# A hybrid short-convolution and SSD trunk: split parts of weight sums kept in DRAM, another order of pairs, two pools exchanged

## The chip, the cores and the metric

The kernel runs on one core of one Trainium2 chip. Time is the device time of an execution in microseconds (us); less is better. Single executions come from the hardware profiler, whose span covers the program from its first to its last instruction.

## The reference

One layer over an input of 2048 positions by 1024 features, float32:

```python
h = rmsnorm(x, norm_mix_w)
proj = einsum("btd,dc->btc", h, w_in)               # 1024 x 5648
u_b, u_c, u_h, z, xbc, dt_raw = split(proj)
y_a = u_b * causal_dwconv(u_c * u_h, short_conv_w)  # 3 taps
xbc = silu(causal_dwconv(xbc, conv_w, conv_b))      # 4 taps
y = ssd_scan(xs, softplus(dt_raw + dt_bias), -exp(a_log), bm, cm) + d_skip * xs
y_b = grouped_rmsnorm(y * silu(z)) * ssd_norm_w
x = x + concat(y_a, y_b) @ w_out                    # 2048 x 1024
h = rmsnorm(x, norm_mlp_w)
x = x + square(relu(h @ w_up)) @ w_down             # 1024 x 4096 x 1024
out = rmsnorm(x, final_norm_w)
```

## The kernel before

**Products.** All large matrix products are made in pairs of output blocks by a scheme with seven products in place of eight (two by two blocks, as Strassen and Winograd have it). `chain` (L272) runs one pair: it goes through the seven products b11, t1, t2, b21, t3, b22, t4, each 4 blocks deep and each block as three matmuls (L297 to L299), because every float32 operand is cut into a high and a low part of type float32r: high times high, high weights times low data, low weights times high data. A product is thus 12 matmuls of 128x512. The results gather in the PSUM tiles px, py and pw and leave through `evict`.

**Weights.** A pair needs four weight operands as (high, low): the block `r0`, the sums `s12` and `s34`, and half of `r1` (`a22`). `combine` (L254) forms the sums on DVE from two loaded blocks (tag `wraw`, 3 buffers) and cuts each with `split_w`: ScalarE (ACT) casts to `whi` (L113), VectorE (DVE) subtracts to `wlo` (L114). `whi` and `wlo` have 4 buffers each, so operand i of the next pair takes the buffer of operand i of this one once PE has done with it. b11 and b21 read operand 0, t1 and t2 operand 1, t3 and b22 operand 2, t4 operand 3. `chain` pulls the next pair's weights from a generator: its loads at t1, two operands after b21, one after b22, one after t4.

**Two halves.** The sequence is worked through as two halves of 1024 positions with the same weights. In the first half (about 75 to 460 us) 20 pairs named in `PAIRS` are projected, and `combine` also stores the two sums (512 KB each) in DRAM, `sums_d`. In the second half (about 460 to 1290 us) come the four output pairs o0 to o3, the 22 pairs of `LATER` (those of `PAIRS`, and z0 and z2), and eight more output pairs. `weights` (L1019) loads r0, s12, s34 and a22 for a pair of `PAIRS`, and cuts all four by `split_w`; z0 and z2 go through `combine`.

**What a pair is followed by.** An x pair has two convolutions of 4 taps (`conv`, three 128x1024 passes on DVE each, and SiLU on ACT), a ch pair a short convolution into a tile `cc`, a b pair a product with two `cc` tiles and sums of its output, a z pair SiLU alone.

**The scan beside it.** `Scan.run` is a generator that yields small steps; `second_half` pulls one to three at each product, so the 32 chunks of the state-space scan run between the products. Its tiles come from the pool `sp1`; `dec` (512 KB, loaded from rd_d at L1613) has one buffer, is changed by ACT (L1673, L127) and DVE (L1679) and read by 16 matmuls into `yd` (L1698). Each change between SiLU and exponent costs ACT a table load.

**Memory and order.** Pools are laid one above the other; a pool that opens where another has closed waits tile by tile for the old tiles' last readers and writers. The first half's pool of temporaries, `pu0`, holds `ea`, `eb` and such (tag `e`) lowest, then other tiles and `cc`, and above it lie the pools of the sums and of raw data. The second half's opens `ut` (4 KB a partition), then `pu1` (tags `cc` and `e`, about 30 KB), then `sp1` (about 27 KB). The first tiles taken from `pu1` are the residual inputs `x` of o0 (L952), to which L985 adds the products. The framework puts the instructions of each engine into an order by its own estimate of when each can run; at run time every engine goes through its list in that order. Nearly all DMAs are issued by SP.

Of the kernel before, what the change touches and what calls it, by code (L numbers as in the profile page):

```python
# [11 lines left out]
F32 = mybir.dt.float32  # L12
# [4 lines left out]
P = 128  # L17
# [6 lines left out]
KD = D // P  # L24
# [15 lines left out]
def trunk(ctx: ExitStack, tc: tile.TileContext, x, x_tok, w_in, w_dt, w_out, w_up, w_down, cvec, hrow, out):  # L40
    nc = tc.nc
# [27 lines left out]
    rd_d = [dram.tile([NC * 16, 2, P], F32, name=f"rd_d{b}") for b in range(NB)]  # L69
    NQ = NF // 2  # L70
    hid_d = [[dram.tile([P, 7, TB], F32, name=f"hid_d{h}_{q}") for q in range(NQ)] for h in range(2)]
    sums_d = {}
    b12_d = dram.tile([P, 3, TB], F32, name="b12_d")
    fin_d = [dram.tile([P, TH], F32, name=f"fin_d{d}") for d in range(KD)]

# [35 lines left out]
    def split_w(raw, eng):  # L111
        hi, lo = wtile(raw.shape[-1])
        nc.scalar.copy(hi, raw)  # L113
        eng.tensor_tensor(out=lo, in0=raw, in1=hi.bitcast(F32), op=ALU.subtract)  # L114
        return hi, lo
# [101 lines left out]
    class Seven:  # L217
# [4 lines left out]
        def raw(self, name):  # L222
            return self.raws.tile([P, 2, TB], F32, tag="uraw", name=name, bufs=4)
# [27 lines left out]
        def sumtile(self, name):  # L251
            return self.us.tile([P, 1024], F32, tag="us", name=name, bufs=2)

        def combine(self, r0, r1, kept=None):  # L254
            w = r0.shape[-1] // 2
            a, b = slice(0, w), slice(w, 2 * w)
            yield split_w(r0, nc.vector)
            s12 = self.sumtile("s12")[:, 0 : 2 * w]
            nc.vector.tensor_tensor(out=s12[:, a], in0=r1[:, a], in1=r1[:, b], op=ALU.add)
            self.sub(s12[:, b], s12[:, a], r0[:, a])  # L260
            if kept is not None:
                nc.sync.dma_start(kept[:, 0], s12)
            yield split_w(s12, nc.vector)
            s34 = self.sumtile("s34")[:, 0 : 2 * w]
            self.sub(s34[:, a], r0[:, a], r1[:, a])
            self.sub(s34[:, b], r0[:, b], s12[:, b])
            if kept is not None:
                nc.sync.dma_start(kept[:, 1], s34)
            yield split_w(s34, nc.vector)
            yield split_w(r1[:, b], nc.vector)  # L270

        def chain(self, groups, ws, ahead, evict, after):  # L272
# [186 lines left out]
    class Proj(Seven):  # L459
# [2 lines left out]
        stored = hm_d  # L462

        PAIRS = "ch0 ch4 b0 x0 x8 ch1 ch5 b1 x2 ch2 ch6 b2 x4 x10 ch3 ch7 b3 x6 z4 z6".split()
        LATER = "x0 z0 x8 z2 x2 ch0 ch4 x10 b0 z4 ch1 ch5 x4 b1 z6 x6 ch2 ch6 b2 ch3 ch7 b3".split()
        FORMER = "o0 o1 o2 o3".split()
        OUTS = "p0 p1 p2 p3 o4 o5 o6 o7".split()
        FIRST = {"z": 24, "x": 32, "b": 0}
# [550 lines left out]
        def weights(self, h, what):  # L1019

            if h == 0:
                sums_d[what] = dram.tile([P, 2, 1024], F32, name=f"sums_{what}_d")
                raws = self.load_cols(w_in, self.cols(what))()
                yield
                yield from self.combine(*raws, sums_d[what])
                return
            w = w_in
            if what[0] == "o":
                w, n = w_out[0], int(what[1])
                what = f"o{n % 4}"  # L1030
                f0, f1 = 2 * (n % 4), 2 * (n % 4) + 1
                if n < 4:
                    sums_d[what] = dram.tile([P, 2, 1024], F32, name=f"sums_{what}_d")
                    raws = self.load_cols(w, (f0, f1))()
                    yield
                    yield from self.combine(*raws, sums_d[what])
                    return
            elif what[0] != "p":
                f0, f1 = self.cols(what)
            raw = lambda n, w=1024: wp.tile([P, 1024], F32, tag="wraw", name=n, bufs=3)[:, 0:w]  # L1040
            if what[0] == "p":
                kept = wy_d[int(what[1])]
                r0, s12, s34 = (raw(n) for n in ("r0", "s12", "s34"))
                for i, t in enumerate((r0, s12, s34)):
                    nc.sync.dma_start(t.rearrange("p (a t) -> p a t", a=2), kept[:, 2 * i : 2 * i + 2])
                last = kept[:, 6]
            else:
                r0 = load_w(w[f0])
                if what not in sums_d:
                    r1 = load_w(w[f1])  # L1050
                    yield
                    yield from self.combine(r0, r1)
                    return
                s12, s34 = raw("s12"), raw("s34")
                nc.sync.dma_start(s12, sums_d[what][:, 0])
                nc.sync.dma_start(s34, sums_d[what][:, 1])
                last = w[f1][:, KD // 2 :]
            yield
            yield split_w(r0, nc.vector)
            a22 = raw("a22", 512)  # L1060
            nc.sync.dma_start(a22 if what[0] == "p" else a22.rearrange("p (k c) -> p k c", c=P), last)
            yield split_w(s12, nc.vector)
            yield split_w(s34, nc.vector)
            yield split_w(a22, nc.vector)
# [810 lines left out]
    with ExitStack() as c1:  # L1875
# [7 lines left out]
        proj_out = Output()  # L1883
        proj.ut = c1.enter_context(tc.tile_pool(name="ut", bufs=1, reuse_waits="tile"))
        with ExitStack() as c2:
            proj.open(c2, 1)
            scan.open(c2, "sp1", 1)
            side = scan.run(0, len(CHUNKS))
            ws = proj.second_half(ws, side)
            for _ in side:  # L1890
                pass
# [105 lines left out]
```

## Time and profile before

| | |
|---|---|
| median of 3 runs | 2617.79 us (2611.75 to 2622.78) |
| the profiled execution | 2613.92 us |
| its span | 2612.1 us |
| mean granted clock of TensorE | 0.996 |
| busy: PE, PE's weight loads, DVE, ACT | 98%, 81%, 76%, 55% |
| moved by DMA | 579.69 MB, 222 GB/s |
| DMA issues of sums in the projections (512 KB) | 40 stores and 40 loads for the 20 pairs |

Engines: PE is TensorE's matmul, PEld its weight load, DVE VectorE, ACT ScalarE, POOL GpSimd, SP the engine that issues DMAs (SPq its queue). An idle time is followed by what ended it. Matmuls overlap: a 128x512 matmul is shown with 0.39 us, and the next one starts 0.23 us after it. A clock of 1.00 is 2.4 GHz, 0.50 is 1.2 GHz.

### The profile page before, as it was taken

The page shows a single profiled execution, that of the slowest core. Times are in us where ns is not written, and L with a number is a line of the kernel's source. Part 1 is how long each engine was busy: PE and PEld are TensorE (multiplying, and loading weights), DVE is VectorE, ACT ScalarE, POOL GpSimd, SP SyncE. Part 2 cuts the span into 40 slices and gives each one's busy share as a digit, 9 for nine tenths or more (in the row PEclk, how much of TensorE's full clock was granted, in tenths as well). Part 3 has the DMA queues.
Part 4 walks back from the last instruction along what each step waited for, and adds up shares of the span by engine and source line. Part 5 has one row for each costly group of instructions (what it writes and reads, how often), then busy time and mean ns, then how long its engine had stood idle before and what let it go on. Part 6 is the DMA issues. An engine that isn't in the chain of part 4 may idle for free.

```text
span 2612.1 us, 33801 instructions
## 1 busy us (share of the span) xinstructions
PE 2564.4 (98%) x11914; PEld 2105.8 (81%) x11914; DVE 1995.9 (76%) x2761; ACT 1427.7 (55%) x2186; POOL 75.4 (3%) x97
## 2 busy tenths in 40 slices
PE   9999999999999999999899999999999999999998
PEld 7888888777877788788788888888888888888887
DVE  7888877787787877888787775755558977877875
ACT  7553345568866665655536555655556444444443
POOL 0011010000000000000000000000000000000001
PEclk9999999999999999999999999999999999999999
DMA  5557856875666756888865674644448766776872
GB/s 214 201 211 274 305 180 230 281 278 165 189 195 212 226 188 182 288 288 309 271 236 213 230 275 147 234 169 141 169 142 277 262 202 205 223 240 220 281 250 77
DMA packets 315544, 579.69 MB, mean 222 GB/s; under 512 B 27632, under 2 KB 158064, under 8 KB 315376
## 3 DMA queue, kind: packets, MB, share of 16 engines
q1 hardware_dynamic: 314944, 577.16, 65.2%
q8 instruction: 93, 1.52, 0.2%
q14 instruction: 75, 0.61, 0.1%
q10 hardware_dynamic: 432, 0.39, 0.0%
HBM read 378.75 MB, written 198.71 MB: 221 GB/s over the span
## 4 chain that ended last, share of the span: by engine, by line
PE 56%; DMA 3%; ACT 2%; DVE 1%; issue 0%; SPq 0%; DVEq 0%; ACTq 0%
PE px L297 10%; PE px L298 10%; PE px L299 10%; PE py L297 5%; PE py L298 5%; PE py L299 5%; PE pw L297 2%; PE pw L299 2%; PE pw L298 2%; PE pm L138 1%; PE pm L139 1%; PE pm L137 1%; DMA rb<-hn_d 1%; DMA dec<-rd_d 0%; DMA yn_d<-y 0%
## 5 line engine op out<-in xcount | busy, mean ns | idle before, releaser
L297 PE MATMUL px<-uh,whi 128*128 128x512 f32 x1864 | 733.6, 394 | 6.4 <-ACT pw L305 3.9
L298 PE MATMUL px<-ul,whi 128*128 128x512 f32 x1864 | 728.6, 391 | 1.8 <-DVE ul L366 1.8
L299 PE MATMUL px<-uh,wlo 128*128 128x512 f32 x1864 | 726.6, 390 | 0.0
L297 PEld LDWEIGHTS px<-uh,whi 128*128 128x128 f32 x1864 | 351.2, 188 | 85.8 <-ACT pw L305 6.0
L298 PEld LDWEIGHTS px<-ul,whi 128*128 128x128 f32 x1864 | 351.2, 188 | 74.5 <-DVE ul L366 3.3
L299 PEld LDWEIGHTS px<-uh,wlo 128*128 128x128 f32 x1864 | 350.9, 188 | 73.6
L297 PE MATMUL py<-uh,whi 128*128 128x512 f32 x932 | 366.6, 393 | 8.2 <-DVE x L985 7.6
L113 ACT CAST whi<-s 128x1024 fp32r<-128x1024 f32 x232 | 242.6, 1046 | 231.3 <-PE py L298 101.7
L298 PE MATMUL py<-ul,whi 128*128 128x512 f32 x932 | 364.0, 391 | 0.6 <-DVE ul L366 0.6
L299 PE MATMUL py<-uh,wlo 128*128 128x512 f32 x932 | 363.7, 390 | 0.0
L114 DVE TENSOR_TENSOR wlo<-s,whi 128x1024 fp32r<-128x1024 f32 x232 | 282.0, 1215 | 70.1 <-ACT whi L113 69.2
L114 DVE TENSOR_TENSOR wlo<-wraw,whi 128x512 fp32r<-128x512 f32 (+3 forms) x213 | 210.9, 990 | 160.0 <-ACT whi L113 159.7
L113 ACT CAST whi<-wraw 128x512 fp32r<-128x512 f32 (+3 forms) x213 | 184.5, 866 | 228.6 <-PE px L298 167.0
L297 PEld LDWEIGHTS py<-uh,whi 128*128 128x128 f32 x932 | 175.2, 188 | 46.7 <-issue 10.3
L299 PEld LDWEIGHTS py<-uh,wlo 128*128 128x128 f32 x932 | 175.2, 188 | 36.7
L298 PEld LDWEIGHTS py<-ul,whi 128*128 128x128 f32 x932 | 175.3, 188 | 36.4 <-DVE ul L366 1.0
L297 PE MATMUL pw<-uh,whi 128*128 128x512 f32 x466 | 182.2, 391 | 0.0
L299 PE MATMUL pw<-uh,wlo 128*128 128x512 f32 x466 | 181.8, 390 | 0.0
L298 PE MATMUL pw<-ul,whi 128*128 128x512 f32 x466 | 181.5, 389 | 0.0
L353 DVE TENSOR_TENSOR ul<-rh,uh 128x1024 fp32r<-128x1024 f32 (+1 forms) x128 | 138.8, 1087 | 49.2 <-ACT uh L352 49.1
L352 ACT CAST uh<-rh 128x1024 fp32r<-128x1024 f32 (+1 forms) x128 | 120.1, 944 | 93.0 <-PE py L299 57.2
L305 ACT COPY pw<-px 128x512 f32<-128x512 f32 x122 | 69.9, 573 | 125.3 <-PE px L299 124.3
(270 smaller groups left out, 3541.7 us busy)
## 6 DMA issues: line engine op xcount, KB each, us to landing
hid_d<-e SPq DMA_DIRECT2D x96, 512.0 KB, 3.8
rh<-hid_d SPq DMA_DIRECT2D x96, 512.0 KB, 4.5
wraw<-w_in SPq DMA_DIRECT2D x68, 512.0 KB, 4.5
wraw<-w_up SPq DMA_DIRECT2D x62, 512.0 KB, 4.3
wraw<-w_down SPq DMA_DIRECT2D x88, 256.0 KB, 4.1
dec<-rd_d SPq DMA_DIRECT2D x32, 512.0 KB, 5.5
x<-x SPq DMA_DIRECT2D x24, 512.0 KB, 6.8
xs_d<-cacc SPq DMA_DIRECT2D x24, 512.0 KB, 3.0
```

The costliest lines, as they stand in the source:

```text
L113: nc.scalar.copy(hi, raw)
L114: eng.tensor_tensor(out=lo, in0=raw, in1=hi.bitcast(F32), op=ALU.subtract)
L137: nc.tensor.matmul(out, whi, hi, start=(k == 0), stop=False)
L138: nc.tensor.matmul(out, whi, lo, start=False, stop=False)
L139: nc.tensor.matmul(out, wlo, hi, start=False, stop=(k == nk - 1))
L297: nc.tensor.matmul(p, hi, h[0], start=bool(first and k == 0), stop=False, **kw)
L298: nc.tensor.matmul(p, hi, h[1], start=False, stop=False, **kw)
L299: nc.tensor.matmul(p, lo, h[0], start=False, stop=(k == len(g) - 1), **kw)
L305: self.copied = nc.scalar.copy(pm[gi]["w"], pm[gi]["x"]).ins
L352: nc.scalar.copy(p[i][0], t)
L353: nc.vector.tensor_tensor(out=p[i][1], in0=t, in1=p[i][0].bitcast(F32), op=ALU.subtract)
```

## The change

Three parts. In the first half the cut parts (high and low) of both sums are stored, four arrays of 512 KB a pair in `parts_d`, where the two sums were stored; the second half loads these into `whi` and `wlo` by DMA, without a cast and a subtract for them. r0 and a22 are loaded ahead together and cut as before. The four output pairs o0 to o3 and z0 and z2 keep what they had. Second, `LATER` names its 22 pairs in another order. Third, in the second half the scan's pool is opened before the pool of temporaries.

```diff
@@ -69,7 +69,7 @@
     rd_d = [dram.tile([NC * 16, 2, P], F32, name=f"rd_d{b}") for b in range(NB)]
     NQ = NF // 2
     hid_d = [[dram.tile([P, 7, TB], F32, name=f"hid_d{h}_{q}") for q in range(NQ)] for h in range(2)]
-    sums_d = {}
+    sums_d, parts_d = {}, {}
     b12_d = dram.tile([P, 3, TB], F32, name="b12_d")
     fin_d = [dram.tile([P, TH], F32, name=f"fin_d{d}") for d in range(KD)]
 
@@ -251,7 +251,15 @@
         def sumtile(self, name):
             return self.us.tile([P, 1024], F32, tag="us", name=name, bufs=2)
 
-        def combine(self, r0, r1, kept=None):
+        def combine(self, r0, r1, kept=None, parts=None):
+
+            def split(s, i):
+                w = split_w(s, nc.vector)
+                if parts is not None:
+                    for j, t in enumerate(w):
+                        nc.sync.dma_start(parts[:, 2 * i + j], t.bitcast(F32))
+                return w
+
             w = r0.shape[-1] // 2
             a, b = slice(0, w), slice(w, 2 * w)
             yield split_w(r0, nc.vector)
@@ -260,13 +268,13 @@
             self.sub(s12[:, b], s12[:, a], r0[:, a])
             if kept is not None:
                 nc.sync.dma_start(kept[:, 0], s12)
-            yield split_w(s12, nc.vector)
+            yield split(s12, 0)
             s34 = self.sumtile("s34")[:, 0 : 2 * w]
             self.sub(s34[:, a], r0[:, a], r1[:, a])
             self.sub(s34[:, b], r0[:, b], s12[:, b])
             if kept is not None:
                 nc.sync.dma_start(kept[:, 1], s34)
-            yield split_w(s34, nc.vector)
+            yield split(s34, 1)
             yield split_w(r1[:, b], nc.vector)
 
         def chain(self, groups, ws, ahead, evict, after):
@@ -462,7 +470,7 @@
         PAIRS = "ch0 ch4 b0 x0 x8 ch1 ch5 b1 x2 ch2 ch6 b2 x4 x10 ch3 ch7 b3 x6 z4 z6".split()
-        LATER = "x0 z0 x8 z2 x2 ch0 ch4 x10 b0 z4 ch1 ch5 x4 b1 z6 x6 ch2 ch6 b2 ch3 ch7 b3".split()
+        LATER = "x0 z0 x8 z2 x2 ch0 x10 ch4 b0 x4 ch1 z4 x6 ch5 b1 z6 ch2 ch6 b2 ch3 ch7 b3".split()
         FORMER = "o0 o1 o2 o3".split()
         OUTS = "p0 p1 p2 p3 o4 o5 o6 o7".split()
         FIRST = {"z": 24, "x": 32, "b": 0}
@@ -1019,10 +1027,10 @@
         def weights(self, h, what):
 
             if h == 0:
-                sums_d[what] = dram.tile([P, 2, 1024], F32, name=f"sums_{what}_d")
+                parts_d[what] = dram.tile([P, 4, 1024], F32, name=f"parts_{what}_d")
                 raws = self.load_cols(w_in, self.cols(what))()
                 yield
-                yield from self.combine(*raws, sums_d[what])
+                yield from self.combine(*raws, parts=parts_d[what])
                 return
             w = w_in
             if what[0] == "o":
@@ -1038,6 +1046,23 @@
             elif what[0] != "p":
                 f0, f1 = self.cols(what)
             raw = lambda n, w=1024: wp.tile([P, 1024], F32, tag="wraw", name=n, bufs=3)[:, 0:w]
+            a22 = lambda: raw("a22", 512)
+            if what in parts_d:
+
+                def ready(i):
+                    w = wtile()
+                    for j, t in enumerate(w):
+                        nc.sync.dma_start(t.bitcast(F32), parts_d[what][:, 2 * i + j])
+                    return w
+
+                r0, r1 = load_w(w[f0]), a22()
+                nc.sync.dma_start(r1.rearrange("p (k c) -> p k c", c=P), w[f1][:, KD // 2 :])
+                yield
+                yield split_w(r0, nc.vector)
+                yield ready(0)
+                yield ready(1)
+                yield split_w(r1, nc.vector)
+                return
             if what[0] == "p":
                 kept = wy_d[int(what[1])]
                 r0, s12, s34 = (raw(n) for n in ("r0", "s12", "s34"))
@@ -1057,7 +1082,7 @@
                 last = w[f1][:, KD // 2 :]
             yield
             yield split_w(r0, nc.vector)
-            a22 = raw("a22", 512)
+            a22 = a22()
             nc.sync.dma_start(a22 if what[0] == "p" else a22.rearrange("p (k c) -> p k c", c=P), last)
             yield split_w(s12, nc.vector)
             yield split_w(s34, nc.vector)
@@ -1883,8 +1908,8 @@
         proj_out = Output()
         proj.ut = c1.enter_context(tc.tile_pool(name="ut", bufs=1, reuse_waits="tile"))
         with ExitStack() as c2:
+            scan.open(c2, "sp1", 1)
             proj.open(c2, 1)
-            scan.open(c2, "sp1", 1)
             side = scan.run(0, len(CHUNKS))
             ws = proj.second_half(ws, side)
             for _ in side:
```

## Rows read from the trace of the kernel before

**Rows 1.** The page: busy us of each engine (share of the span) xinstructions.

```profile
PE 2564.4 (98%) x11914; PEld 2105.8 (81%) x11914; DVE 1995.9 (76%) x2761; ACT 1427.7 (55%) x2186; POOL 75.4 (3%) x97
```

**Rows 2.** Busy time by stretch: start:end, length, engines, clock, DMA share, GB/s.

```profile
100.00:450.00 350.00, 349.71 (x1543) 289.07 (x1541) 288.74 (x359) 160.10 (x199) 33.80 (x37) 1.00 0.65 234
468.00:480.00 12.00, 11.25 (x39) 9.06 (x40) 6.51 (x10) 2.71 (x3) 0.00 (x0) 0.75 0.65 242
530.00:1060.00 530.00, 511.24 (x2651) 416.31 (x2650) 427.57 (x648) 370.87 (x673) 25.77 (x37) 0.99 0.65 203
540.00:560.00 20.00, 20.00 (x92) 16.27 (x90) 14.94 (x16) 12.70 (x16) 0.00 (x0) 1.00 1.03 401
560.00:570.00 10.00, 7.47 (x38) 5.49 (x37) 9.83 (x16) 9.56 (x19) 0.73 (x1) 1.00 0.61 236
600.00:622.00 22.00, 17.11 (x81) 13.56 (x80) 15.86 (x37) 20.71 (x32) 0.00 (x0) 0.84 0.55 174
690.00:1050.00 360.00, 348.65 (x1833) 286.64 (x1832) 289.43 (x429) 236.01 (x456) 15.15 (x25) 1.00 0.65 201
1130.00:1250.00 120.00, 117.50 (x595) 96.48 (x594) 100.99 (x145) 72.28 (x132) 0.00 (x0) 1.00 0.89 301
```

**Rows 3.** Waits at 455:470, all engines, then SP's queue: us, times, longest.

```profile
PE py L297 <- DVE x L985: 5.0, 1, 5.0
...
SPq L952 <- DMA sz_d<-eb: 5.2, 1, 5.2
```

**Rows 4.** Timeline at the seam: start, us, engine, line, operation, idle before.

```profile
452.23 1.21 DVE L114 TENSOR_TENSOR wlo<-s,whi 128x1024 fp32r<-128x1024 f32 x1
...
455.77 2.09 SPq L358 DMA_DIRECT2D ul<-y_d  x3
463.16 0.81 SPq L952 DMA_DIRECT2D x<-x  x2
...
467.91 0.69 DVE L985 TENSOR_TENSOR x<-py,x 128x512 f32<-128x512 f32 x1 [1.52 <-DMA x<-x]
...
473.58 0.59 PE L299 MATMUL px<-uh,wlo 128*128 128x512 f32 x1
474.00 0.40 PE L297 MATMUL px<-uh,whi 128*128 128x512 f32 x1
474.24 0.40 PE L298 MATMUL px<-ul,whi 128*128 128x512 f32 x1
```

**Rows 5.** Waits of PE and DVE at 530 to 1060 us.

```profile
PE yd L1698 <- DVE dec L1679: 6.8, 3, 3.8
PE pss L1734 <- DVE ssq L1731: 5.9, 5, 1.9
...
DVE stmp L1729 <- ACT stmp L1728: 15.1, 10, 4.1
```

**Rows 6.** Groups at 530 to 1060 us: busy us, mean ns, idle before, releasers.

```profile
L113 ACT CAST whi<-s 128x1024 fp32r<-128x1024 f32 x43 | 45.1, 1048 | 43.5 <-PE py L298 33.4 <-PE pw L298 8.2 <-DMA dec<-rd_d 1.4
...
L114 DVE TENSOR_TENSOR wlo<-s,whi 128x1024 fp32r<-128x1024 f32 x43 | 52.5, 1221 | 13.2 <-ACT whi L113 13.0 <-DMA dec<-rd_d 0.2
```

**Rows 7.** Timeline around 600 us, ACT and PE.

```profile
598.32 1.03 ACT L113 CAST whi<-s 128x1024 fp32r<-128x1024 f32 x1
...
611.33 1.98 PE L1698 MATMUL yd<-dec,stmp 128*64 128x128 f32 x16 [3.85 <-DVE dec L1679]
```

**Rows 8.** DMA issues, 530:1060 (two), then 1130:1250: count, KB, median landing.

```profile
dec<-rd_d SPq DMA_DIRECT2D x22, 512.0 KB, 5.5
...
s<-sums_x_d SPq DMA_DIRECT2D x12, 512.0 KB, 5.3
...
dec<-rd_d SPq DMA_DIRECT2D x4, 512.0 KB, 6.0
```

**Rows 9.** Waits of SP's queue at 530 to 1060 us.

```profile
SPq L1061 <- DVE wlo L114: 25.9, 10, 9.2
SPq L1745 <- DVE y L1739: 25.2, 5, 9.7
```

## Prediction

> **What bounds the kernel now.** I read the page first: PE is busy for 2564.4 us, 98% of the span of 2612.1 [rows 1]. PE is the bound. Nothing saved on DVE, ACT or SP counts unless it closes one of PE's gaps, and all gaps together are 47.7 us. Next I cut the span into stretches. Where the first half runs (100 to 450 us) PE stands still for 0.3 us in 350: there the change has nothing to win [rows 2]. Where the second half reads stored sums (530 to 1060 us) PE stands still for 18.8 us in 530, with DVE busy 81% and ACT 70%. The gaps lie in spots: 2.5 us at 560 to 570, 4.9 us at 600 to 622, and 11.3 us in small pieces at 690 to 1050 [rows 2].
>
> The one large gap ahead of these is the seam between the halves. There PE waits 5.0 us for the add into `x` (L985) [rows 3]; the add waits for the load of `x`, which SP had held for 5.2 us until the store `sz_d<-eb` landed [rows 3, 4]. The loaded tile thus lies on memory which that store still read. Behind the gap the granted clock is 0.75 as a mean over 12 us [rows 2]: matmuls start 0.42 us apart until 474.0 and 0.24 us apart after it [rows 4], the low level (1.2 GHz) and the high one (2.4 GHz). The reader is to see that such a gap is paid twice, once standing and once slow. A mean of 0.75 between 0.5 and 1 is 6 of 12 us at the low level; 0.8 of them still lie in the gap, and half of the other 5.2 is lost: 2.6 us.
>
> The waits then name the owners. In 530 to 1060 PE waits mostly for scan work: `dec` from DVE 6.8 us, `ssq` from DVE 5.9 us [rows 5]. These come late because DVE and ACT are full and work in order. ACT alone stood 33.4 + 8.2 us in front of casts of sums, whose output buffer PE had not yet released, with the scan's steps behind them [rows 6].
>
> **The change part by part, in the first half.** All 20 pairs store four arrays of 512 KB where two were stored: 40 stores more, 40 x 0.524 MB = 21 MB. Their cover is the DMA engines' room: 65% busy at 234 GB/s, and 21 MB over 350 us is 60 GB/s, some 17 points of share by the same row [rows 2]. The stores wait for the split instead of the sum, so SP stands longer by one cast and one subtract (1.05 + 1.22 us [rows 6]). Behind them on SP is the next pair's weight load, needed more than five products later; a product is 12 matmuls of 0.23 us, 2.7 us. I cost this part at 0. Without that cover it would be 21 MB at the 401 GB/s that a full stretch reached [rows 2], 52 us over 20 pairs.
>
> **In the second half.** For each of the same 20 pairs two casts (128x1024, 1.05 us) leave ACT and two subtracts (1.22 us) leave DVE [rows 6]: 42 us of ACT and 49 us of DVE, whose busy time in 530 to 1060 falls from 427.6 to about 379. Four loads of 512 KB stand for two, again 21 MB, 40 GB/s on top of 203. The other order of pairs moves an x pair (six long DVE passes) between pairs that have none, and removes nothing. I give it no price of its own; it lies inside the bounds of the gaps.
>
> *560 to 570 us (2.5 us).* The second half's input arrives just before, with the DMA at 1.03 share and 401 GB/s [rows 2]. The first pair with stored parts loads 1.05 MB more there: 2.6 us later. Its two casts and subtracts leave ACT and DVE in the same stretch, 2.1 and 2.4 us earlier. I take 0, between +2.6 and -2.5.
>
> *600 to 622 us (4.9 us standing, and slow matmuls).* The clock's mean of 0.84 is 7 us at the low level; some 2 of them fall into the gap itself, and half of the other 5 is lost: 2.5, together 7.4. PE waits 3.85 us of it for `dec` [rows 7], and ACT is busy 20.7 of 22 us [rows 2], with two of the casts that go (one of them at 598.32 [rows 7]) in the 20 us before `dec`. Taking 2.1 us off ACT brings `dec` forward by as much, and a gap of under 3 us may not cost the clock: 2.1 + 2.5 = 4.6, which I take, between 0 and 7.4.
>
> *690 to 1050 us (11.3 us).* 43 casts of sums in 530 us are 21.5 pairs of 24.7 us [rows 6], so 14.6 pairs lie here, and 14.6 x 2.4 = 35 us leave DVE, ten points of 360. What waits behind a full queue shrinks, what waits for a chain of small scan steps does not. I take half, 5.6, between 0 and 11.3.
>
> *The seam.* With the scan's pool opened first, the pool of temporaries starts some 27 KB higher. By the tile sizes the `x` tiles then lie on tiles of the first half's convolutions and of its last sums; the last reader of those is the split that ends at 453.4 us [rows 4]. SP ends its loads at 457.9 us and is free for `x` then, 5.2 us earlier. Landing took 4.7 us (463.2 to 467.9 [rows 4]), so `x` would be there at about 462.6, as long before the adds as PE now waits. The full price of the gap is 5.0 + 2.6 = 7.6. Next late are the weights of o1, whose loads SP issues behind `x`: they move forward by the 5.2 us alone. I take 6.0, between 0 and 7.6. The scan's first loads now meet the memory of `eb`, but the code begins them at o0's fifth product, after that store has landed.
>
> *What the loads cost.* `dec` lands in 5.5 us at a DMA share of 0.65 and in 6.0 us at 0.89 [rows 2, 8]. 21 MB are some 13 points more, 0.3 us for each of 22 loads. 22 x 0.3 = 6.6 us is the upper bound, with 2.6 us of the first pair 9; below it is 0, since a late `dec` need not be felt by PE. I take 3.
>
> A page speaks against this term. The Trainium skill, "HBM Reference", section Latency, puts an access at 0.2 us on average and 2 us under high load. By that, as an estimate, each `dec` could come up to 1.8 us later, and with the same third of the upper bound the term would be 14 and the sum near -2; the two rows on `dec` show far less than that.
>
> Sum: -6.0 - 4.6 - 5.6 + 3 = -13.2 us. The profiled execution took 2613.92 us (span 2612.1 and 1.8 around it), which gives 2600.7. It lay 3.9 us under the median of the three runs shown, 2617.79; on that scale, which I give, it is 2604.6, so 2604.5.
>
> **Rivals.** *Only the seam gives.* The scan's waits are chains of small steps, and PE meets them at any load of DVE; for it speaks that DVE itself stood 15.1 us for ACT between two small steps [rows 5]. Then -6 + 3 = -3: 2615. Chance 0.18.
>
> *The seam's wait only changes hands.* The weights of o1 take its place and PE stands as long, with the other terms kept: -7, 2611. Against it: SP is free from 457.9 on. Chance 0.05.
>
> *All gaps close.* If queueing is the whole cause: 7.6 + 7.4 + 11.3 + 2.5 = 28.8, 2589; with 3 for the loads 2592. For it speaks how full DVE and ACT are. Chance 0.17.
>
> *Slower: the parts come late.* A stored part can only be loaded once PE has left its buffer, five products ahead of its use, 13.6 us. Before, the sum was on chip by then, and only a cast and a subtract were left. A load of sums lands in 5.3 us [rows 8] and the second is issued up to 1 us after the first, so SP may be late by 13.6 - 6.3 = 7.3 us. SP's longest wait for a store there is 9.7 us [rows 9]. Behind such a one PE would stop for 2.4 us and, with as much lost by the clock as at the seam, pay 5.0. Three of them eat the gain, six make the kernel slower by more than can be told; with seven it is -13 + 35 = +22: 2640. For it speaks that ACT's 41.6 us of waiting in front of the casts [rows 6] become waits of SP, with the scan's loads behind them. Against it: 25.9 us of SP's present waits, for the raw buffers of just these weights, go at the same time [rows 9]. Chance 0.12.
>
> **How the numbers follow.** My forecast has 0.48, with its own range 2597 to 2611. The range for 8 in 10 takes in the two cases above it and most of the closed gaps: 2590 to 2619. What can be told from no change is 0.5%, 13 us: under 2604.7 counts as faster. The forecast lies on that edge; the closed gaps (0.17) and some two thirds of the forecast (0.33, as its bounds reach further down than up) give 0.50 faster; the rest of it (0.15) and the two rivals of smaller gain (0.23) give 0.38 same; 0.12 slower.
>
> **What would show it.** Seam right: no wait of SP for `sz_d<-eb` ahead of `x`, PE's gap there under 2 us, clock 1.00. Casts right: 40 `whi` casts of sums fewer on ACT and the gap at 600 to 622 under 3 us. Loads right: they land in 5 to 7 us and no matmul waits for them. It is wrong if PE waits for a DMA of stored parts more than twice, if the first half's gaps grow past 2 us, or if the gaps in 690 to 1050 stay at 11 us with DVE ten points less busy.

## The result and the profile after

The changed kernel takes 2625.36 us (median of 10 runs, 2623.58 to 2629.10), the kernel before 2615.08 us beside it (10 runs). The ratio is 1.0038, interval 1.0028 to 1.0048: 9.9 us slower, 7 to 13, where 13 us faster was forecast. It is less than the 0.5% named as the bound of no change, but the interval leaves no doubt of its sign, and the time lies 6 us above the forecast's range. The profiled spans say the same: 2621.9 against 2612.1 us.

The page's busy times of the changed kernel answer to [rows 1], and its line of DMA bytes follows.

```profile
PE 2572.3 (98%) x11914; PEld 2108.3 (80%) x11914; DVE 1954.1 (75%) x2721; ACT 1386.0 (53%) x2143; POOL 60.7 (2%) x97
...
DMA packets 327066, 621.67 MB, mean 237 GB/s; under 512 B 28912, under 2 KB 159344, under 8 KB 326896
```

The casts and subtracts are gone as planned: ACT is busy 41.7 us less, DVE 41.8. The bytes came as planned too: 42 MB more than the 579.69 of before. PE has the same 11914 matmuls; it is busy 8 us longer and stands only 1.9 us longer. By the granted clock of the two traces, 25.3 us of the span lie at the low level, against 18.4 before; half of the difference, 3.4 us, is lost by it. What makes up the rest of the 8 us was not found.

The stretches of [rows 2], in the changed kernel (columns as there):

```profile
100.00:450.00 350.00, 348.55 (x1535) 287.67 (x1534) 287.25 (x358) 157.44 (x197) 34.89 (x37) 1.00 0.77 283
...
468.00:480.00 12.00, 9.18 (x28) 7.16 (x29) 8.29 (x12) 3.91 (x5) 0.00 (x0) 0.72 0.82 315
530.00:1060.00 530.00, 510.87 (x2617) 414.29 (x2617) 381.56 (x601) 325.85 (x618) 11.25 (x37) 0.99 0.76 238
...
560.00:570.00 10.00, 9.66 (x48) 7.07 (x47) 7.36 (x10) 7.26 (x13) 0.00 (x0) 1.00 1.03 413
600.00:622.00 22.00, 17.25 (x81) 13.82 (x80) 14.94 (x39) 20.37 (x35) 0.00 (x0) 0.84 0.76 269
690.00:1050.00 360.00, 346.73 (x1801) 283.45 (x1800) 253.70 (x396) 199.14 (x415) 7.03 (x26) 0.99 0.79 240
```

In 530 to 1060 us DVE and ACT are each busy some 45 us less than before, and PE stands as long as before (19.1 us). At 600 to 622 nothing moved: same 17.2 us of PE, same clock. At 690 to 1050 the gaps grew from 11.3 to 13.3 us, with DVE ten points less busy: the sign of being wrong that the prediction had named. What rose is the DMA share, from 0.65 to 0.76.

Where the time went shows when the same matmul is set against its time in the kernel before. This is worked out from the starts of every 84th matmul of a large product (one pair); the columns are us behind before, a minus is ahead. Some of the experiments stand beside it, for later.

```
before at   after   pools   high parts  + copies   copies     order,
                    alone   loaded      of low     at `dec`   scan first
  452.7     +2.0    +1.8    +1.1        +0.4       -0.2       +0.8
  479.5     +3.2    -0.9    +0.7        +0.8       -0.7       +0.6
  548.6     +4.7    +0.3    +1.2        +0.3       +7.9       +1.8
  599.4     +2.2    +2.1    -1.6        -0.5      +13.6       +1.7
  656.9     +2.5    +3.3    -7.3        -0.7       +7.8       +2.6
  800.3     +8.7    +3.8    -7.0        +5.2       +9.7       +5.3
  899.9    +10.0    +6.2    -7.1        +5.7      +10.7       +2.3
 1039.1    +10.8    +7.4    -6.6        +7.0      +12.5       +1.1
 1178.8     +8.2    +9.3   -10.1        +3.9      +16.1       -1.9
 1246.5     +8.8    +9.7    -8.5        +6.2      +26.4       -1.4
 2564.0     +9.8    +7.7    -7.0        +7.5      +22.2       -1.1
```

The changed kernel loses 2 us in the first half and 7.5 between 657 and 900 us. There is no wait of PE for a stored part anywhere.

**The seam.** SP no longer stands in front of `x`, yet the gap is the 5.0 us of [rows 3], once more. First the waits at 455 to 475 us in the changed kernel, then SP's timeline, then DVE's:

```profile
PE py L305 <- DVE x L993: 5.0, 1, 5.0
```

```profile
455.19 2.25 SPq L366 DMA_DIRECT2D ul<-y_d  x4
457.53 0.60 SPq L937 DMA_DIRECT2D sz_d<-eb  x1
458.23 1.57 SPq L366 DMA_DIRECT2D ul<-y_d  x3
459.97 1.66 SPq L960 DMA_DIRECT2D x<-x  x2
```

```profile
466.46 1.23 DVE L374 TENSOR_TENSOR ul<-ul,uh 128x1024 fp32r<-128x1024 f32 x1 [0.63 <-ACT uh L373]
467.94 2.04 DVE L374 TENSOR_TENSOR ul<-ul,uh 128x512 fp32r<-128x512 f32 x3 [0.26 <-ACT uh L373]
469.98 0.69 DVE L993 TENSOR_TENSOR x<-py,x 128x512 f32<-128x512 f32 x1
```

`x` is issued at 460.0 instead of 463.2, but behind seven loads of `ul`, with the DMA engines full (share 1.02 at 460 to 472 us), and its two loads now take 9.9 us each where before took 4.7 [rows 4]. Nor would an earlier `x` help: before, DVE stood 1.52 us for it [rows 4]; now the first `x` lands at 469.9 us, just as the subtracts of `ul` end, DVE goes from these into the add without a pause, and those subtracts had waited for their own loads.

**At 600 us.** PE's gaps there and what DVE did just before, in the changed kernel:

```profile
610.53 0.54 PE L1680 MATMUL ptx<-ident,xd 128*128 128x128 f32 x4 [2.14 <-DVE state L1739]
...
613.42 1.97 PE L1723 MATMUL yd<-dec,stmp 128*64 128x128 f32 x16 [1.52 <-DVE dec L1704]
```

```profile
608.59 0.69 DVE L267 TENSOR_TENSOR s<-wraw 128x512 f32<-128x512 f32 x1 [2.04 <-DMA wraw<-w_in]
609.20 0.68 DVE L1764 TENSOR_TENSOR y<-y,ssq 128x512 f32<-128x512 f32 x1
609.80 0.68 DVE L1739 COPY state<-st 128x512 f32<-128x512 f32 x1
```

The reader follows it upward: PE waits for the scan's `state`; DVE makes it two places behind a sum of raw weights, which stood 2.04 us for its load. That load (`wraw<-w_in`) was issued at 599.6, behind four part loads issued from 595.6 on, and took 9.0 us. The casts are gone from ACT; a late load holds DVE instead. In the kernel before, `state` stood ahead of that sum in DVE's list, and the sum waited for nothing:

```profile
605.82 0.69 DVE L1714 COPY state<-st 128x512 f32<-128x512 f32 x1 [0.17 <-PE st L139]
...
607.70 0.68 DVE L259 TENSOR_TENSOR s<-wraw 128x512 f32<-128x512 f32 x1
```

So it takes two things to make this chain, the late load and the new order of DVE's list.

**In 690 to 1050 us** the chain is the same, through ACT. ACT's timeline, and PE's largest gap:

```profile
890.28 0.99 ACT L1698 ACTIVATE dec<-dec,dd 128x128 f32<-128x128 f32 x3 [3.14 <-DMA dec<-rd_d]
...
893.92 0.62 ACT L1753 ACTIVATE stmp<-y 128x512 f32<-128x512 f32 x1
```

```profile
895.95 0.46 PE L1759 MATMUL pss<-ssq,ones_r 128*128 128x128 f32 x2 [3.23 <-DVE ssq L1756]
```

`dec`, issued at 881.5 behind two part loads, took 8.7 us; the square that `ssq` needs stands behind `dec` in ACT's order. ACT's waits for `dec` grew from 27.2 us to these, at 530 to 1060 us:

```profile
ACT dec L1698 <- DMA dec<-rd_d: 53.8, 17, 9.1
```

Landing times at 530 to 1060 us (issues, KB, median us), first before, then after; `dec` was 5.5 before [rows 8]:

```profile
wraw<-w_in SPq DMA_DIRECT2D x23, 512.0 KB, 4.2
...
a<-w_in SPq DMA_DIRECT2D x20, 256.0 KB, 3.2
```

```profile
wraw<-w_in SPq DMA_DIRECT2D x23, 512.0 KB, 5.1
dec<-rd_d SPq DMA_DIRECT2D x21, 512.0 KB, 6.5
...
a<-w_in SPq DMA_DIRECT2D x20, 256.0 KB, 5.1
```

(`a` is the tile of a22.) Not every kind came later: `y<-sz_d` lands in 3.5 us before and 3.4 after, `xd<-xs_d` in 3.7 and 3.8.

### The profile page after: what moved, and what is told of

It is laid out like the page before. It is cut to its first block, busy times and chain, and to the rows that moved or that the text cites. A ratio compares the mean times of both kernels' runs of the same rounds, so it can differ in the third digit from the quotient of the medians.

```text
span 2621.9 us, 33864 instructions
## 1 busy us (share of the span) xinstructions
PE 2572.3 (98%) x11914; PEld 2108.3 (80%) x11914; DVE 1954.1 (75%) x2721; ACT 1386.0 (53%) x2143; POOL 60.7 (2%) x97
## 4 chain that ended last, share of the span: by engine, by line
PE 79%; DMA 9%; DVE 6%; ACT 4%; issue 2%; SPq 1%; DVEq 0%; ACTq 0%
PE px L305 14%; PE px L306 13%; PE px L307 13%; PE py L305 6%; PE py L306 6%; PE py L307 6%; PE pw L307 3%; PE pw L305 3%; PE pw L306 3%; DMA dec<-rd_d 3%; PE pm L138 1%; PE pm L139 1%; PE pm L137 1%; PE pm L523 1%; ACT dec L1698 1%
## 5 line engine op out<-in xcount | busy, mean ns | idle before, releaser
L113 ACT CAST whi<-s 128x1024 fp32r<-128x1024 f32 x192 | 200.6, 1046 | 187.1 <-PE pw L306 70.9
L114 DVE TENSOR_TENSOR wlo<-s,whi 128x1024 fp32r<-128x1024 f32 x192 | 233.0, 1214 | 60.1 <-ACT whi L113 59.3
```

## The experiments

Every ratio is against runs of the kernel before on the same chip. Theory A: the second array loaded for each sum costs more than the casts it replaces, through loads that land later. Rivals: the order of the pairs costs, the pools cost, or a part can only be loaded when PE has left its buffer, whatever its bytes. One more rival was left out: with a second transfer the framework puts the engines' instructions into another order, and that order was held fixed in no run. "Bytes or buffers" comes back to it.

### Each edit alone

The pools alone:

```diff
-            proj.open(c2, 1)
             scan.open(c2, "sp1", 1)
+            proj.open(c2, 1)
```

> The kernel before with the two lines of the seam exchanged (the scan's pool opened ahead of the temporaries), nothing else. Traffic theory (the transfers in the queue ahead of the load of `x` set the seam): the gap of PE at 470 us stays between 3 and 5 us, the owner of the wait is the load of `x` that is issued earlier but lands later; time of before within 3 us. Theory of the prediction (the seam's wait hung on the store of `eb`): the gap shrinks under 2 us and the time falls by 6 us.

2623.88 us, ratio 1.0020 (1.0007 to 1.0034): 5 us slower, which neither side expected. At the seam it did a part of what the prediction said: PE is 2.7 us better off between 453 and 480 us. The gap is 3.5 us, within the 3 to 5 of the traffic theory.

```profile
PE py L297 <- DVE x L985: 3.5, 1, 3.5
```

By 599 us that is lost again (+2.1 in the table), and 5 us more by 1040. PE, ACT, DVE and SP go through the same lists of instructions as before until the end of these projections, so what differs in that stretch is where the tiles lie and when things happen. Which of the two costs the 5 us was not found. Without a byte or an instruction more, `dec` lands later than before's 5.5 us [rows 8] here too:

```profile
dec<-rd_d SPq DMA_DIRECT2D x21, 512.0 KB, 6.0
```

The order of the pairs alone:

> The kernel before with the new order of the second half's pairs, nothing else. Traffic theory: no more than 3 us from before, either way. Rival (the order itself costs): 4 us or more slower, with the loss between 690 and 1050 us, where the order differs.

2614.50 us, ratio 0.9992 (0.9982 to 1.0003): nothing that can be told. The order is not the cause.

The parts alone, old order and old pools:

> The parts stored and loaded, with the old order of pairs and the old order of the pools. Traffic theory: 6 to 12 us slower than before, as much as the whole change, with `dec` landing 1 us later than before's 5.5 and PE waiting for the scan's steps behind it. Theory of the prediction: faster than before by 5 to 8 us (its terms for 600 to 622 and 690 to 1050 less that of the loads), so that the loss must come from the order or the pools.

2621.18 us, ratio 1.0016 (1.0007 to 1.0025): 4 us slower, below what theory A expected, on its side of zero. In this kernel the casts that go are worth less than what came with the parts.

### The casts without the second array

```diff
-                    for j, t in enumerate(w):
-                        nc.sync.dma_start(parts[:, 2 * i + j], t.bitcast(F32))
+                    nc.sync.dma_start(parts[:, 2 * i], w[0].bitcast(F32))
...
+                    hi = wp.tile([P, 1024], F32R, tag="whi", name="whi", bufs=4)
+                    nc.sync.dma_start(hi.bitcast(F32), parts_d[what][:, 2 * i])
+                    return hi, hi
```

> The whole change, but of each sum only the high part is stored and loaded, and the products use the high tile in place of the low one: the low part of the stored sums is left out of the result. Casts and subtracts are gone as in the changed kernel, while the bytes stored and loaded are those of the kernel before. Traffic theory: `dec` lands in 5.5 us again, and the time is 5 to 13 us under before (the terms of the prediction without the loads' cost), so 15 to 23 us under the changed kernel. Rival (the parts come late because a part can only be loaded when PE has left its buffer, whatever the bytes): as slow as the changed kernel, within 3 us.

2607.88 us, ratio 0.9960 (0.9946 to 0.9974): 10.5 us under before, 17 to 20 under the changed kernel (by medians and by ratios). With the same matmuls, and casts and subtracts gone, the edit gives back the second array alone (the lists of the engines change with it, as shown below). The page's bytes are those of before, 579.70 MB. `dec` lands in 5.9 us, not in the 5.5 that was expected.

### Stores or loads

Both parts stored, only the high one loaded:

> The whole change with both parts of each sum stored in the first half, but only the high one loaded in the second, where it stands in for the low part too: the low part of the stored sums is left out of the result. It splits the 17 us between the run with the high parts only (2607.9) and the changed kernel into stores and loads. Theory (the loads lengthen the queue in the second half): the stores cost 1 to 4 us, so 2609 to 2612, and the loads the rest. Rival (the stores of the first half delay what the second half starts from): 2618 or more.

2605.67 us, ratio 0.9966 (0.9955 to 0.9976). The 21 MB of extra stores in the first half cost nothing that can be told. The 21 MB of extra loads in the second, with all that comes with them, cost 1.0038 - 0.9966 = 0.0072, 19 us with 4 either way. The column "high parts loaded" shows where: 600 to 657 us, and 657 to 900. Its windows at 600 to 622 and 690 to 1050 us:

```profile
600.00:622.00 22.00, 20.29 (x107) 16.61 (x106) 14.65 (x29) 21.34 (x45) 1.28 (x2) 1.00 0.50 162
690.00:1050.00 360.00, 352.03 (x1840) 289.19 (x1839) 257.61 (x400) 199.54 (x421) 5.96 (x24) 1.00 0.67 202
```

This is what the prediction's casts promised: at 600 us PE stands 1.7 us at full clock, where it stood 4.9 at 0.84, and the gaps at 690 to 1050 fall from 11.3 to 8.0. The loads that the changed kernel delays land sooner here, but the raw weights, at 4.9 us, are nearly as late as there (5.1):

```profile
dec<-rd_d SPq DMA_DIRECT2D x22, 512.0 KB, 5.8
...
a<-w_in SPq DMA_DIRECT2D x19, 256.0 KB, 3.6
```

### Bytes or buffers

The run above also leaves the low buffers free, so it is not yet the bytes alone. Here each high load has a copy of the low part from memory to memory behind it:

```diff
+                    to = dram.tile([P, 1024], F32, name=f"copy_{what}_{i}_d")
+                    with behind(last.ins):
+                        nc.sync.dma_start(to, parts_d[what][:, 2 * i + 1])
```

> The run with both parts stored and only the high ones loaded (2605.7), and right behind each of the 40 high loads a copy of the low part from memory to memory: the bytes of the changed kernel, while the low buffers on chip stay as free as without them. The low part of the stored sums is left out of the result as there. Theory (the bytes of the second load cost the 20 us): 2615 or more, over half of the way back to the changed kernel's 2625. Rival (what costs is the second load's claim on the low buffers: SyncE waits until PE has left one, with the scan's loads behind): the copies cost 5 us or less, so 2611 or under.

2623.79 us, ratio 1.0023 (1.0013 to 1.0032). Bytes that no instruction reads bring back 15 of the 19 us. The stretches at 600 and 690 us look like those of the changed kernel again:

```profile
600.00:622.00 22.00, 17.23 (x81) 13.88 (x81) 13.39 (x30) 20.85 (x36) 0.00 (x0) 0.84 0.66 224
690.00:1050.00 360.00, 345.94 (x1804) 282.71 (x1803) 252.76 (x395) 198.87 (x417) 6.10 (x24) 1.00 0.79 240
```

So is the chain, in DVE's timeline:

```profile
606.01 0.69 DVE L267 TENSOR_TENSOR s<-wraw 128x512 f32<-128x512 f32 x1 [2.25 <-DMA wraw<-w_in]
606.62 0.68 DVE L1766 TENSOR_TENSOR y<-y,ssq 128x512 f32<-128x512 f32 x1
607.22 0.68 DVE L1741 COPY state<-st 128x512 f32<-128x512 f32 x1
```

The other 4 us may be the buffers or the runs' spread.

So the buffers are not needed for most of the loss. But the run does not separate the bytes from the order of the lists. The framework orders each engine's list by its own estimate, and a second transfer for each sum, part or copy, changes that estimate. Counted from the traces between 460 and 1290 us, without the part loads and the copies themselves, the lists of the run with the high parts loaded and of the changed kernel agree until about 550 us and then differ at some 55 places on PE and some 70 on each of ACT, DVE and SP. Those of the changed kernel and of the run with the copies differ at 2, 9, 12 and 17 places. The copies bring back the changed kernel's bytes and its lists together, and all that the copies cost lies behind 550 us. Of the 16.8 us that lie between the changed kernel and the run with the high parts loaded at the end of the table, 3.5 are there by 549 us, when the first part load has just been issued (547.6 us); these are not the loads'.

How much of the 19 us is bytes in flight and how much the new order stays open. For the bytes speaks that the same loads land later in both kernels with a second transfer than in the run without: `dec` 6.5 and 6.4 us against 5.8, `a22` 5.1 and 4.7 against 3.6. For the order speaks the sum at 600 us, which has `state` behind it where it had stood ahead, and that another order alone, with the bytes kept, is worth 5 to 6 us under "Place in the queue". A third of the 19 us, 6.5, is the clock: 25.3 us at the low level in the changed kernel and 12.3 in the run with the high parts loaded, half of it lost.

### Place in the queue

If a load is late because of what stands ahead of it in SP's queue, its place should matter. Two copies of 512 KB beside each load of `dec` in the kernel before, once ahead and once behind:

```diff
+            with behind(self.copies(n, last.ins)):
                 nc.sync.dma_start(t["dec"], rd_d[b][r0 : r0 + HG, 0, :].partition_broadcast(P))
...
+        def copies(self, n, last):
+            for j in range(2):
+                to = dram.tile([P, KD, P], F32, name=f"copy{n}_{j}_d")
+                with behind(last):
+                    last = nc.sync.dma_start(to, w_in[j]).ins
+            return last
```

> The kernel before with two copies of 512 KB from memory to memory issued just ahead of each of the scan's loads of `dec` (44 copies, 23 MB, as much as the 40 part loads). Nothing on chip is touched by them. Theory (place in line): `dec` lands 2 to 3 us later than before's 5.5, and each such delay is felt almost whole, so 25 to 60 us slower. Rival (fuller DMA engines, wherever the bytes stand in the queue): as slow as the run with the copies behind `dec`, within 8 us.

> The same 44 copies issued just behind each load of `dec`, everything else as in the run above. Theory (place in line): `dec` lands as before (5.5 to 6 us), only what stands behind it comes later, 0 to 15 us slower. Rival (fuller DMA engines): 20 us slower or more, and within 8 us of the run with the copies ahead.

2634.82 and 2635.02 us, ratios 1.0068 (1.0051 to 1.0085) and 1.0064 (1.0051 to 1.0078): 17 us each. There are 64 copies in all, 33.6 MB, 44 of them at 530 to 1060 us. Landing times of `dec` at 530 to 1060, 460 to 545 and 1130 to 1320 us, copies ahead first, then behind:

```profile
dec<-rd_d SPq DMA_DIRECT2D x21, 512.0 KB, 5.7
dec<-rd_d SPq DMA_DIRECT2D x4, 512.0 KB, 7.7
dec<-rd_d SPq DMA_DIRECT2D x6, 512.0 KB, 7.7
```

```profile
dec<-rd_d SPq DMA_DIRECT2D x21, 512.0 KB, 6.0
dec<-rd_d SPq DMA_DIRECT2D x4, 512.0 KB, 5.5
dec<-rd_d SPq DMA_DIRECT2D x6, 512.0 KB, 5.8
```

The first row of each says nothing about place. In the run with the copies ahead, SP's timeline has both copies right ahead of `dec` at 10 of the 32 loads only, the first four and the last six; at the other 22 they were issued 4 to 43 us earlier, 2 to 28 places ahead, and all but one pair had landed when `dec` was issued. Copies behind stand one to four places behind `dec` throughout. At the 10 loads place matters for the landing: 7.8 us by the median with the copies right ahead, 5.7 with them behind (later in 8 of the 10), 5.4 in the kernel before. So there that part of the theory holds.

It does not matter for the time. With the copies ahead 13 us are lost between 480 and 599 us and 9 between 1179 and 1202, with the copies behind 14 and 10 (the column of the table): what gains by its place has other loads behind it that lose. These are in or near the stretches where before's DMA share is 1.03 and 0.89 already [rows 2]. Between 657 and 1039 us the copies cost 3.5 us and 4.7, where the second array costs 7.6 (changed kernel against high parts loaded). So a number of bytes has no one price. The lists of both runs differ from before's at 54 places or more on each engine, so these losses too are bytes and order together.

The scan's step put ahead of the weights' step at each product, which changes the list of every engine, SP's too:

```diff
+                early = getattr(self, "early", False)
+                if early:
+                    after(name)
                 if ahead is not None:
...
-                after(name)
+                if not early:
+                    after(name)
```

> The changed kernel with the scan's step put ahead of the next weights' step behind each product of the pairs in the second half, so that a load of the scan is issued ahead of the part loads of the same product. Theory (place in line): 5 to 15 us under the changed kernel, so 2610 to 2620, with `dec` landing under 6 us. Rival (fuller engines, or the parts then come late): within 3 us of the changed kernel, or slower.

2627.48 us, ratio 1.0040 (1.0026 to 1.0054): no gain, as the rival had it; `dec` lands in 6.2 us, not under 6.

The same with the new order of pairs, without parts and with the old pools, and the same in the kernel before as it was:

> The kernel before with the new order of pairs and the same exchange of scan's step and weights' step: the control of the run above without the parts, and a candidate to beat the kernel before. Theory (place in line): sums are half the bytes, so less to win, 0 to 6 us under the 2614.5 of the order alone. Rival: no change, or slower because the casts of the weights stand behind the scan's work on ScalarE.

> The kernel before, old order of pairs, with the scan's step put ahead of the weights' step behind each product: half of the run that came out at 2610.8. If that gain is the scan's place: 2610 to 2614. Rival (it was the order of the pairs, 2614.5 alone, and chance): 2615 to 2618.

2610.78 us, ratio 0.9978 (0.9967 to 0.9990), and 2612.08 us, ratio 0.9979 (0.9970 to 0.9989). Both beat the kernel before, by 5 to 6 us, and so both kernels of the study: the exchange of the two steps does it, and the order of the pairs adds nothing that can be told. `dec` lands no earlier for it (6.2 and 5.7 us), and which of the moved instructions gives the gain was not found. PE's busy time at 690 to 1050 us rises to 352.5 and 351.1 of 360 us, from 348.65 [rows 2].

### Another queue

`dec` issued by GpSimd, in two halves, with GpSimd's halo copies moved to DVE:

```diff
-            nc.sync.dma_start(t["dec"], rd_d[b][r0 : r0 + HG, 0, :].partition_broadcast(P))
+            for i in range(2):
+                hs = slice(i * HG // 2, (i + 1) * HG // 2)
+                nc.gpsimd.dma_start(t["dec"][:, hs], rd_d[b][r0 : r0 + HG, 0, :][hs].partition_broadcast(P))
```

> The changed kernel with the loads of `dec` (in two halves each) issued by GpSimd instead of SyncE, and GpSimd's four kinds of halo copies moved to VectorE so that GpSimd has nothing else to wait for there. Theory (place in line): off SyncE's queue `dec` lands in 5 us or less, ScalarE's wait for it in 530 to 1070 us falls from 55 us to under 25, and the time is 5 to 10 us under the changed kernel, 2616 to 2621. Rival (the DMA engines are simply fuller): `dec` lands as late as in the changed kernel (6.5 us), and the time stays within 3 us of it or rises by what the copies cost VectorE.

> The kernel before with the same move of `dec` to GpSimd and of the halo copies to VectorE: the control of the run above. Theory (place in line): with half the part traffic there is less to win, 0 to 4 us under the kernel before. Rival (fuller engines): no change but for the copies on VectorE, 0 to 3 us slower.

2753.64 and 2739.25 us, ratios 1.0543 and 1.0482: 138 and 124 us lost. It tests nothing of the theory, because the second half was not issued until the first had landed. GpSimd's waits at 530 to 1060 us, in the kernel before with this edit:

```profile
POOL dec L1615 <- DMA dec<-rd_d: 69.5, 14, 6.7
```

In all 32 pairs the second half is issued 0.3 us after the first has landed. Each half lands in 5.0 us, so `dec` is whole some 5 us later than before, 32 times. 124 us over 32 is 3.9 us a load; as an estimate, with the copies on DVE and a new order of the lists in it, PE feels most of a `dec` that is late by so much.

The two loads of `x` for o0 issued by GpSimd, with the pools exchanged:

```diff
-                self.residual(order[0], b)
+                self.residual(order[0], b, nc.gpsimd)
```

> The kernel before with the pools exchanged, and the two loads of `x` for o0 issued by GpSimd, whose queue holds nothing else then, instead of SyncE behind the loads of `ul`. Theory (at the seam PE waits for a load that stands in line behind the seven `ul` loads of SyncE's queue): `x` lands before 463 us, the gap of PE at the seam falls from 3.5 us (the pools alone) to under 1 us, and PE reaches 480 us some 4 to 8 us ahead of the kernel before. Rival (all queues share the same full DMA engines): `x` lands no earlier than 467 us and the gap stays at 3 us or more. For the whole time the first says 2606 to 2616 if the lead is kept, and about 2617 if the second half's input load at 540 to 560 us takes it back.

2622.51 us, ratio 1.0026 (1.0016 to 1.0036). One `x` was issued at 414.9 us, the other at 455.8, and it landed 7.7 us later, at 463.5: ahead of the loads of `ul`, and still the gap is 5.8 us. DVE's timeline shows who is next:

```profile
468.49 2.04 DVE L366 TENSOR_TENSOR ul<-ul,uh 128x512 fp32r<-128x512 f32 x3 [0.26 <-ACT uh L365]
470.45 0.68 DVE L985 TENSOR_TENSOR x<-py,x 128x512 f32<-128x512 f32 x1
```

The add stands behind the subtracts of `ul` on DVE, and these behind the `ul` loads. At 460 to 472 us the DMA share is 1.01. So `x` was never alone; the seam ends when SP's whole batch of loads has landed.

### The change without the pools

> The changed kernel without the exchange of the pools: parts and new order of pairs. If the three edits add up (parts +4, order -2, pools +7 by the runs of each alone): 2617 to 2620, and the exchange of the pools costs 5 to 8 us in company too. Rival (the pools cost only by chance of timing in the kernel before): within 3 us of the changed kernel's 2625.

2623.20 us, ratio 1.0023 (1.0013 to 1.0034), between the two expectations. The pools cost 0.0015 in company and 0.0020 alone, each with an interval of about 0.0014: 4 to 5 us, by a mechanism that stays open.

## Why the prediction was wrong, step by step

**What bounds it.** PE, and its gaps in spots: right.

**The casts and subtracts (600 to 622 us, -4.6; 690 to 1050, -5.6).** A gain of this size is there, and visible only with the second array away. There the clock at 600 is 1.00, and PE gains 3.2 us in that window and 3.4 in the other. For the sum, the first run with high parts only has the pools' +5.2 and the order's -2 in its -10.5, so the casts, with the new lists, are worth some 13.6, with 4 us either way, against 10.2 forecast. Its place is right for one term of two. By the table the run with the high parts loaded gains 5.7 us between 599 and 657 us; between 657 and 1039 it loses 0.7, where the pools alone lose 4.1, so at most some 3 of the 5.6 were gained there. That the sum came out near is luck in part: 2.8 us more were gained between 549 and 599, which the forecast had put at 0. ACT's 41.6 us of waiting in front of the casts [rows 6] did not vanish: it went to other ACT instructions that follow PE (`whi` of a22 22.4 us, `stmp` 19.8 and 11.8).

**What the loads cost (+3, between 0 and 9).** This is the step that failed. Measured: 19 us, the new order of the lists included. I priced one load, `dec`, by a mean of 0.3 us and let PE feel a third. By medians `dec` became later by 1.0 us, `a22` by 1.9, the raw weights by 0.9. Against the run with the high parts loaded, which loads no more bytes than before, it is 0.7, 1.5 and 0.2: most of the raw weights' delay is not the second array's. And ACT and DVE work in order: a load of weights that no matmul waits for, `wraw<-w_in`, holds DVE for 2 us with the scan's `state` behind it. That `state` would come to stand behind it was not in my term at all; I took the lists as they were. The room that I counted on, a share of 0.65, is a mean; within it, four part loads issued in 4 us took the share at 594 to 608 us from 0.58 to 0.84 (0.75 with the high parts alone), just where the scan's step was next. By the Trainium skill, "HBM Reference", section Latency, the term had come out at 14. The delay of `dec` lies between its 1.8 us and my 0.3, and the time is nearer to its side. No run here shows memory latency itself as the cause.

**The seam (-6.0, between 0 and 7.6).** SP was set free as forecast, and the memory too; the gap stayed at 5.0 us in the changed kernel and fell to 3.5 with the pools alone. The step that failed is "next late are the weights of o1": next were the `ul` loads in front of `x`, 5 us of full DMA, and DVE's order. So the rival of small chance, that the wait only changes hands, was the right one for the seam, with another successor. In place of the gain the exchange costs 4 to 5 us, behind the seam and by a mechanism that stays open.

**First half (0).** 2 us by 453 us in the changed kernel, and between 0.4 and 3.6 in the five others with the same stores; those without extra stores spread from -0.3 to +2.0. So 0 was right within what can be told: PE stands 1.45 us at 100 to 450, under the 2 us named.

**560 to 570 us (0).** PE stands 0.3 us there against 2.5 before [rows 2], and 0.6 instead of nothing in the 20 us ahead. The gap went, as the lower bound had it; by the table the changed kernel makes good 2.5 us between 549 and 599 us, of 4.7 that it was behind by then.

**Order of pairs (no price).** Right: 0.9992.

**The slower rival** had the sign and not the cause: no matmul waits for a stored part, and the time is 15 us below its 2640. What it got right is SP, which now stands in front of the part loads for buffers that PE has not left (25.0 and 21.8 us in the two largest groups at 530 to 1060).

**The sum.** The pools' +5.2, the order's -2.1 and the parts' +4.2 make +7.3, against +9.9 measured (7 to 13). The sum forecast, -13.2, misses 23 us: 16 of it in the loads and 11 at the seam and the pools, less 3 by which the casts gave more and 2 of the order; what is left is under the spread of the runs. The terms are taken from runs whose lists differ, so that they add up is no proof of each.

## What to carry to other kernels

Before trading engine work for bytes, look at what else loads in the same stretch, and at which in-order engine stands next at a load that comes late: here a load that no matmul waits for held the scan's step. The same 21 MB cost nothing that can be told as stores in the first half and 19 us as loads in the second, at nearly the same DMA share of 0.76 to 0.78, so a share does not give the price. That the slack of the loads beside them makes the difference is my reading; it was not tested. When a transfer is added or taken away, compare the engines' lists of both kernels as well: where they differ, a difference in time is not the bytes alone. Look in the timeline whether an edit that is to put one transfer ahead of another did so. And where a wait hangs on the last of a batch of loads, moving one of them forward only shows the next.

## What the runs showed of the hardware that was not expected

- With two copies of 512 KB issued right ahead of it in the same queue, `dec` landed in 7.8 us (median of 10 loads), with the copies right behind it in 5.7, without them in 5.4. The two runs cost the same 17 us all the same.
- A load issued by GpSimd at 455.8 us shared the full DMA engines with SP's: 7.7 us for a load that took 8.1 in SP's queue. The Trainium skill, "DMA: Bandwidth & Descriptors", section "Issuing engines are not separate DMA queues", says that DMAs of different engines run on the same 16 DMA engines and interleave; this row agrees.
- Of two broadcast loads of 256 KB issued by GpSimd in a row, the second was issued only when the first had landed, 32 times out of 32 (69.5 us of such waiting at 530 to 1060 us).
